# One reciprocal per head, another order of the first casts, product 5's weights by way of DRAM, two queues for the last stores

## The chip, the cores and the metric

The kernel runs on one core of a Trainium2 chip. The metric is the device time of one execution in microseconds (us), given as the median of several runs; lower is better. A profiled execution is recorded apart from those runs and has a time of its own.

## The reference

One residual layer for 512 tokens of width 1024 in float32. The normalised input goes through one combined projection; its parts feed two attention branches and two gates; the branches are projected, gated, summed and projected once more, and a normalisation ends the layer.

```python
h = rmsnorm(x, norm_g)
(q_lat, c_kv, k_rope, z_a, q_b, k_b, v_b, z_b,
 q_idx, k_idx, w_idx, gate_a, gate_b) = split(h @ w_in)      # 1024 x 5576
# branch a: 8 heads, latent queries (rank 384), latent keys and values (rank 256), rotary part
q  = rmsnorm(q_lat, g_q_lat) @ w_uq ;  kv = rmsnorm(c_kv, g_kv_lat) @ w_ukv
y_a = softmax(chunk_causal(q k^T * scale)) v * silu(z_a)
# branch b: 8 heads; an indexer scores the keys, each query keeps the 128 best admissible ones
score = sum_h relu(q_idx k_idx^T) * w_idx ;  idx = top_k(score, 128)
y_b = softmax(q_b k_b[idx]^T * scale + rel_bias) v_b[idx] * silu(z_b)
merged = sigmoid(gate_a) * (y_a @ w_o_a) + sigmoid(gate_b) * (y_b @ w_o_b)
out = rmsnorm(x + merged @ w_out, final_g)
```

## The kernel before

**Numbers in two parts.** Each float32 operand of an important product is split into a high part, rounded to the matmul's input type fp32r, and a low part, the rest. A product is three matmuls: high by high, high by low, low by high (`mm3`). The helpers record the instructions, so many steps share a line: matmuls L395, transposes of probabilities L412, casts to the high part L297 on ScalarE (ACT), low parts and other two-tensor steps L323 on VectorE (DVE) or L325 on GpSimd (POOL), activations L306 (ACT), scalings by a value per row L353 (DVE), L356 (POOL) or L306 (ACT), DMAs of the SyncE queue (SP) L422.

**Weights.** Every weight comes from DRAM once, through SP's one queue in program order, into a raw tile (four of 128x1024 float32, named `raw`; at the start `s_er`). ACT makes its high part and DVE or POOL its low part in one of 73 slots of 128x512 (`s_w`, `s_wo`, and others by their use); then the raw tile is free for the next load.

**The order of the work.** A scheduler of the kernel's own, the class `Flow`, decides it when the program is built. The work is written as threads (Python generators) that yield a `Step` (engine options, reads, writes), a `Get` (a buffer of a pool) or an `Until` (a condition). Each thread has a priority. `Flow.run` puts down, again and again, the step that can start first by a cost model, with a bias by priority, and where a step has several engines, the one on which it ends first. The model has a line for SP's DMAs: an issue time, the time the data takes on the shared transfers, a landing time. Small random nudges are drawn from a seed, `DRAW`. What is put down is the program order of each engine; at run time engines wait for one another by semaphores only.

**The stages.** (1) x arrives transposed in blocks `s_x`; ACT scales each by the input's norm gains and makes the high part `s_xg`, DVE the low one. The first weight blocks (`s_er`: the latent and index columns q and kv) are cast to `s_w`, and PE multiplies them as the blocks of x arrive. Fifteen matmuls of zeros run ahead of the first. (2) The other columns of the projection in an order given by the string `QUEUE`, with the normalised input `s_h`. Meanwhile DVE finds the top 128 keys of each query (16 rounds of max and replace for three tiles), and the a-heads' attention runs between PE's products. (3) The b-heads in the same way, their operands moved to their partitions by DMAs (`s_op`, `qhi`, `s_pair` on the way). (4) The gated projections, and last the output projection by w_out in seven products of sums and differences of blocks instead of eight, in the order 1, 7, 2, 6, 5, 4, 3. Products 5 and 7 multiply differences of w_out's blocks: `out_job` loads a pair of blocks as one raw tile of 512 KB, subtracts (`s_wsum`), casts and makes the low part (`s_wo`), four times for product 5. (5) `finish` adds x (`s_xr`), multiplies by the final gain (`s_fg`), sums squares, and `scale_out` scales the halves of each row tile (`s_rg`) and stores them.

**A head.** `mla_head` (a) and `dsa_head` (b) have four row tiles of 128 queries with 128, 256, 384 and 512 keys. For each, the function `soft` finds the negative row maximum, exponentiates on ACT with the row sum in `accum`, and normalises:

```python
def normalise(p, mx, engs=None):
    yield Step([("DVE", 0.07, lambda: nc.vector.reciprocal(mx.tile[:, 3:4], mx.tile[:, 2:3]))], [mx], [mx])
    step = scale_by(p, p, mx[:, 3:4], engs or NORM)
```

`NORM` is DVE or POOL (a-heads), `NORM_B` DVE or ACT (b-heads). When all tiles of a head are scaled, `attend` transposes them by matmuls with an identity (L412), makes high and low parts (`s_ph`) and multiplies by the values (`vv`).

## Time and profile before

| | |
|---|---|
| median of 3 runs | 428.33 us (428.06 to 428.80) |
| the profiled execution's own time | 430.56 us |
| its span in the trace | 428.8 us |
| mean granted TensorE clock | 0.991 of full speed |
| TensorE (PE) busy | 416.8 us, 97% of the span, 2313 matmuls |
| VectorE (DVE) busy | 379.1 us, 88% |
| ScalarE (ACT) busy | 261.1 us, 61% |
| GpSimd (POOL) busy | 120.2 us, 28% |
| bytes moved by DMA | 65.89 MB, 154 GB/s on the mean |

Times in the rows of the profile are in us from the start of the span unless marked ns. A row of a timeline has start, length, engine, line, operation, output tile <- input tiles, shape, how many, and in brackets how long the engine was idle before and which step ended that. PE is the matmul stream, PEld its weight loads, SPq and ACTq the DMAs that these engines issue. A matmul's length is modelled; a busy PE isn't always one at its peak.

### The profile page before, as it was taken

How to read it: one execution, taken by the hardware profiler on the slowest of the kernel's cores; microseconds unless marked ns; L12 is line 12 of the kernel's file. 1: busy time of each engine (PE TensorE's matmuls, PEld its weight loads, DVE VectorE, ACT ScalarE, POOL GpSimd, SP SyncE). 2: the span in 40 equal slices, each digit the busy share in tenths (PEclk: the TensorE clock that was granted, in tenths of full speed). 3: DMA queues.
4: the chain of work that ended last, by engine and by line, in shares of the span. 5: the costliest groups of instructions: out<-in, count | busy, mean ns of one | idle time of the engine just before them, and what ended most of it. 6: DMA issues, size and time to landing. Idle time of an engine off the chain costs nothing.

```text
span 428.8 us, 7187 instructions
## 1 busy us (share of the span) xinstructions
PE 416.8 (97%) x2313; PEld 365.4 (85%) x2313; DVE 379.1 (88%) x851; ACT 261.1 (61%) x589; POOL 120.2 (28%) x141
## 2 busy tenths in 40 slices
PE   7999999999999999999999999999999999999994
PEld 5999978888888888878899888988898888888883
DVE  3679999999999999998777897998799867999985
ACT  5876877576373838449462768584499534436623
POOL 1045767466264678200000001110000002010552
PEclk8999999999999999999999999999999999999997
DMA  8973144635555363182443425515432897356405
GB/s 260 396 265 113 52 153 127 185 113 134 132 124 161 106 179 98 39 222 73 137 135 112 148 98 131 160 49 187 117 125 78 270 336 266 128 160 234 148 0 196
DMA packets 30277, 65.89 MB, mean 154 GB/s; under 512 B 4648, under 2 KB 5688, under 8 KB 30240
## 3 DMA queue, kind: packets, MB, share of 16 engines
q1 hardware_dynamic: 29264, 64.08, 48.3%
q0 software_dynamic: 832, 1.22, 1.0%
q8 instruction: 18, 0.29, 0.3%
q14 instruction: 19, 0.16, 0.1%
q10 hardware_dynamic: 144, 0.13, 0.1%
HBM read 50.49 MB, written 4.21 MB: 128 GB/s over the span
## 4 chain that ended last, share of the span: by engine, by line
PE 74%; DVE 13%; DMA 4%; ACT 4%; issue 2%; POOL 0%; SPq 0%; POOLq 0%; ACTq 0%; DVEq 0%
PE ps L395 66%; PE ps L412 4%; DVE s_w L323 2%; ACT s_p L306 2%; DMA raw<-w_gb 2%; DVE s_ph L323 1%; ACT s_w L297 1%; DMA qhi<-qhi 1%; DMA s_x<-xT 1%; DVE raw L323 1%; PE ps L798 1%; DVE s_tmp L323 1%; PE ps L1461 1%; PE ps L1460 1%; DVE s_y L323 1%
## 5 line engine op out<-in xcount | busy, mean ns | idle before, releaser
L395 PE MATMUL ps<-s_h,s_w 128*128 128x512 f32 (+1 forms) x732 | 169.7, 378 | 0.7 <-ACT s_pair L297 0.7
L395 PEld LDWEIGHTS ps<-s_h,s_w 128*128 128x128 f32 x732 | 127.9, 189 | 22.8 <-ACT s_pair L297 0.9
L297 ACT CAST s_w<-raw 128x512 fp32r<-128x512 f32 (+3 forms) x124 | 71.7, 593 | 24.6 <-DVE raw L323 15.9
L325 POOL TENSOR_TENSOR s_w<-raw,s_w 128x512 fp32r<-128x512 f32 (+2 forms) x38 | 46.0, 1214 | 106.8 <-ACT s_w L297 105.3
L323 DVE TENSOR_TENSOR s_w<-raw,s_w 128x512 fp32r<-128x512 f32 (+2 forms) x86 | 58.2, 689 | 5.7 <-ACT s_w L297 4.9
L395 PE MATMUL ps<-s_ys,s_w 128*128 128x512 f32 x192 | 43.7, 389 | 0.0
L395 PEld LDWEIGHTS ps<-s_ys,s_w 128*128 128x128 f32 x192 | 36.0, 188 | 7.5
L395 PE MATMUL ps<-s_w,s_xg 128*128 128x328 f32 (+1 forms) x192 | 34.0, 333 | 0.6 <-DVE s_w L323 0.3
L395 PEld LDWEIGHTS ps<-s_w,s_xg 128*128 128x128 f32 x192 | 32.5, 195 | 1.2 <-DVE s_w L323 0.7
L395 PE MATMUL ps<-s_wo,s_mg 128*128 128x512 f32 (+1 forms) x156 | 33.0, 373 | 0.0
L395 PEld LDWEIGHTS ps<-s_wo,s_mg 128*128 128x128 f32 x156 | 27.6, 188 | 5.2
L306 ACT ACTIVATE s_p<-s_p,sm 128x128 f32<-128x128 f32 (+3 forms) x53 | 27.5, 541 | 7.2 <-DVE sm L1539 6.1
L323 DVE TENSOR_TENSOR s_ph<-ps,s_ph 128x384 fp32r<-128x384 f32 (+1 forms) x48 | 27.5, 593 | 3.6 <-ACT s_ph L297 3.6
L306 ACT ACTIVATE s_p<-ps,sm 128x128 f32<-128x128 f32 (+3 forms) x32 | 16.8, 527 | 17.0 <-DVE sm L1442 16.4
L325 POOL TENSOR_TENSOR s_p<-s_bias,mask 128x384 f32<-128x384 f32 (+1 forms) x5 | 4.3, 886 | 78.1 <-DVE s_w L323 71.8
L297 ACT CAST s_ph<-ps 128x384 fp32r<-128x384 f32 (+1 forms) x48 | 23.8, 521 | 4.0 <-PE ps L412 3.8
L821 DVE MATCH_REPLACE8 mask<-sm,mask 128x384 f32<-128x384 f32 (+2 forms) x48 | 25.8, 542 | 0.0
L820 DVE MAX8 sm<-mask 128x8 f32<-128x384 f32 (+2 forms) x48 | 25.5, 548 | 0.1
L395 PE MATMUL ps<-s_ph,vv 128*128 128x512 f32 (+3 forms) x128 | 25.4, 324 | 0.0
L412 PE MATMUL ps<-ident,s_p 128*128 128x128 f32 x160 | 23.8, 273 | 0.7 <-DVE s_p L353 0.7
L412 PEld LDWEIGHTS ps<-ident,s_p 128*128 128x128 f32 x160 | 19.2, 140 | 4.2 <-DVE s_p L353 1.1
L395 PEld LDWEIGHTS ps<-s_ph,vv 128*128 128x128 f32 x128 | 20.4, 189 | 1.8
(195 smaller groups left out, 769.0 us busy)
## 6 DMA issues: line engine op xcount, KB each, us to landing
raw<-w_out SPq DMA_DIRECT2D x18, 512.0 KB, 3.9
s_op<-s_op SPq DMA_DIRECT2D x36, 128.0 KB, 4.1
raw<-w_ga SPq DMA_DIRECT2D x8, 512.0 KB, 4.0
raw<-w_gb SPq DMA_DIRECT2D x8, 512.0 KB
raw<-w_o SPq DMA_DIRECT2D x16, 256.0 KB, 4.1
s_x<-xT SPq DMA_DIRECT2D x8, 256.0 KB
s_xn<-x SPq DMA_DIRECT2D x8, 256.0 KB, 5.6
bias_scratch<-s_sig SPq DMA_DIRECT2D x8, 256.0 KB, 2.0
```

What stands on the lines that cost most here:

```text
L297: nc.scalar.copy(dst.ap, src.ap)
L306: nc.scalar.activation(dst.ap, src.ap, func, **kw)
L323: opts.append(("DVE", 0.07 + 0.00104 * x.n, lambda: nc.vector.tensor_tensor(dst.ap, x.ap, y.ap, op=op)))
L325: opts.append(("POOL", 0.15 + 0.0021 * x.n, lambda: nc.gpsimd.tensor_tensor(dst.ap, x.ap, y.ap, op=op)))
L395: nc.tensor.matmul(ps.ap, l.ap, r.ap, start=start and i == 0, stop=stop and i == len(pairs) - 1, skip_group_check=more)
L412: nc.tensor.transpose(d.ap, s.ap, ident.tile)
L798: yield pe(0.005 + n / 2400, [ps.all], [qs[h].all, ks[0].all], lambda: nc.tensor.matmul(ps.tile[:, :n], qs[h].tile[:96, TOK[i]], ks[0].til ...
L820: yield Step([("DVE", t, lambda: nc.vector.max(m8.tile, work.tile))], [m8], [work])
L821: yield Step([("DVE", t, lambda: nc.vector.match_replace(work.tile, m8.tile, work.tile, MARK))], [work], [m8])
L1460: nc.tensor.matmul(o, q0[0:96], k1[0:96], start=False, stop=False)
L1461: nc.tensor.matmul(o, q1[0:96], k0[0:96], start=False, stop=True)
```

## The change

Four edits and the constants that go with them.

- `Sums` takes the place of `normalise`. A head's four row sums go to four columns of one small tile, one reciprocal of 128x4 is made when the fourth sum is there, and then each row tile is scaled. `NORM` gets ACT as a third engine.
- The scheduler's cost model counts transfers as 1.36 times as long (`SLOW`) until the modelled 7.3 us, and costs a DMA issued by ACT apart; the seed `DRAW` goes from 0 to 55. The program comes out in another order: on ACT the first weight cast (q) stands ahead of the first block of x, and the next one (kv) ahead of the second block; on DVE the low parts follow that order. SP's loads of the first microseconds keep their order. PE has the same matmuls with other neighbours.
- `make` loads product 5's four pairs of blocks after head b1, as single blocks of 256 KB into `raw` slots (`s_raw`), subtracts in place, makes the high and the low part and stores the eight results to DRAM. `fetch_made` loads them back, 256 KB each, when product 6's weights are ready. Product 5 leaves the list of `out_job`.
- `scale_out` of the last row tile (t = 1) has three pieces: half 0 by DVE and SP; columns 128 to 512 of half 1 scaled by ACT and stored by a DMA that ACT issues itself; its columns 0 to 128 by DVE and SP.

In counts: DVE goes from 802 instructions to 758 (64 reciprocals of 128x1 become 16 of 128x4); ACT keeps 505 and POOL 146; SP goes from 255 to 275 and ACT issues one DMA more.

```diff
@@ -220,14 +220,19 @@
 
                 self.free["SP"] = s + 0.05
                 self.hw = max(self.hw, s) + (0.65 if step.ins and step.outs else 0.475)
-                self.dma = max(self.dma, self.hw + 0.65) + dur
+                self.dma = max(self.dma, self.hw + 0.65)
+
+                self.dma += dur * (SLOW if self.dma < 7.3 else 1.0)
                 end = self.dma + (2.2 if step.ins and step.outs else 1.0) + step.late
             else:
                 self.free[eng] = end = s + dur
                 if self.shares(step, eng):
                     self.port = end
-                if step.moves:
-                    self.dma = max(self.dma, end + (1.0 if eng == "POOL" else 0.8)) + step.moves
+                if step.moves and eng == "ACT":
+
+                    end += 1.8 + step.moves
+                elif step.moves:
+                    self.dma = max(self.dma, end + 1.0) + step.moves
                     end = self.dma + 1.0
             for b in step.ins:
                 b.r = b.reads[eng] = max(b.r, end)
@@ -240,7 +245,7 @@
 RAW_LAG = {"DVE": 0.125, "POOL": 0.1, "ACT": 0.1}
 BIAS = 0.01
 NUDGE = 0.01
-DRAW = 0
+DRAW = 55
 TC_ARGS = {}
 
 
@@ -1415,11 +1420,38 @@
         put(ps, t)
         done.add((br, h))
 
-    def normalise(p, mx, engs=None):
-        yield Step([("DVE", 0.07, lambda: nc.vector.reciprocal(mx.tile[:, 3:4], mx.tile[:, 2:3]))], [mx], [mx])
-        step = scale_by(p, p, mx[:, 3:4], engs or NORM)
-        step.abias = NORM_BIAS if engs else 0.0
-        yield step
+    class Sums:
+
+
+        def __init__(self, group):
+            self.group, self.have, self.done, self.left, self.buf = group, 0, False, len(group), None
+
+        def at(self, i):
+            if self.buf is None:
+                self.buf = yield Get(SMALL)
+            c = i - self.group[0]
+            return self.buf[:, c : c + 1]
+
+        def normalise(self, i, p, engs=None):
+            n = len(self.group)
+            self.have += 1
+            yield Until(lambda: self.have == n)
+            if i == self.group[0]:
+                t = self.buf.tile
+                yield Step([("DVE", 0.07, lambda: nc.vector.reciprocal(t[:, 4 : 4 + n], t[:, 0:n]))], [self.buf], [self.buf])
+                self.done = True
+            else:
+                yield Until(lambda: self.done)
+            c = 4 + i - self.group[0]
+            step = scale_by(p, p, self.buf[:, c : c + 1], engs or NORM)
+            step.abias = NORM_BIAS if engs else 0.0
+            yield step
+            self.left -= 1
+            if not self.left:
+                put(self.buf)
+
+    def sums_of_head():
+        return {i: s for s in (Sums(g) for g in GROUPS) for i in s.group}
 
     def prob_tiles(cls, cap):
         s = []
@@ -1434,17 +1466,17 @@
         yield Until(lambda: ("a", h, 0) in operands and ("a", h, 1) in operands)
         (qh, ql), (kh, kl) = operands["a", h, 0], operands["a", h, 1]
         slots, probs = yield from prob_tiles("p", 6)
-        ready = set()
+        ready, sums = set(), sums_of_head()
 
         def soft(i, ps):
             n = P * (i + 1)
             mx = yield Get(SMALL)
             yield Step([("DVE", 0.07 + 0.00104 * n, lambda: nc.vector.tensor_reduce(
                 mx.tile[:, 1:2], ps.tile[:, :n], op=ALU.max, axis=AX.X, negate=True))], [mx], [ps])
-            yield act(probs[i], ps[:, :n], AF.Exp, bias=mx[:, 1:2], scale=1.0, accum=mx[:, 2:3])
-            put(ps)
-            yield from normalise(probs[i], mx)
-            put(mx)
+            den = yield from sums[i].at(i)
+            yield act(probs[i], ps[:, :n], AF.Exp, bias=mx[:, 1:2], scale=1.0, accum=den)
+            put(ps, mx)
+            yield from sums[i].normalise(i, probs[i])
             ready.add(i)
 
         for i in ORDER:
@@ -1530,7 +1562,7 @@
         yield Until(lambda: ("b", h, 0) in operands and ("b", h, 1) in operands and h in bases)
         qb, (kh, kl) = operands["b", h, 0], operands["b", h, 1]
         slots, probs = bases[h]
-        ready = set()
+        ready, sums = set(), sums_of_head()
 
         def soft(i, ps):
             n = P * (i + 1)
@@ -1543,9 +1575,10 @@
             yield step
             put(ps)
 
-            yield act(p, p, AF.Exp, bias=mx[:, 1:2], scale=-1.0, accum=mx[:, 2:3])
-            yield from normalise(p, mx, NORM_B)
+            den = yield from sums[i].at(i)
+            yield act(p, p, AF.Exp, bias=mx[:, 1:2], scale=-1.0, accum=den)
             put(mx)
+            yield from sums[i].normalise(i, p, NORM_B)
             ready.add(i)
 
         for i in ORDER:
@@ -1705,6 +1738,48 @@
             src = a["w_out"][4 * h + 2 * g + c]
         Job(src, [512, 512], None, prep=prep)
 
+
+    store = nc.dram_tensor("made_scratch", (len(MADE) * 8, P, S), F32, kind="Internal").ap()
+
+    def made(product, k, part):
+        return store[8 * MADE.index(product) + 2 * k + part]
+
+    def make():
+        yield is_done(("b", 1))
+        for product in MADE:
+            h, g = {1: (0, 0), 2: (0, 1), 3: (1, 1), 5: (1, 0)}[product]
+            for k in range(4):
+                raw = yield slot("raw")
+                yield dma(raw.all, w_block(h, g, k))
+                if product == 5:
+                    other = yield slot("raw")
+                    yield dma(other.all, w_block(0, 0, k))
+                    yield soon(tt(raw.all, raw.all, other.all, ALU.subtract, BOTH))
+                    put(other)
+                hi = yield slot("wo")
+                lo = yield slot("wo")
+                yield act(hi.all, raw.all)
+                yield soon(lo_part(lo.all, raw.all, hi.all))
+                put(raw)
+                for part, t in enumerate((hi, lo)):
+                    yield dma(made(product, k, part), t.all.f)
+                put(hi, lo)
+                done.add(("made", product, k))
+
+    def fetch_made():
+        for product in MADE:
+            first = {5: (6, 3), 3: (4, 3), 2: (7, 3), 1: None}[product]
+            for k in range(4):
+                yield is_done(("made", product, k), "projections")
+                yield Until(lambda: first is None or first in right or first in used)
+                pair = []
+                for part in range(2):
+                    t = yield slot("wo", 32)
+                    yield dma(t.all.f, made(product, k, part))
+                    pair.append(t)
+                right[product, k] = tuple(pair)
+
+    used = set()
     xr, fg = {}, {}
 
     def final_loads():
@@ -1761,10 +1836,21 @@
         done.add(("sum", t))
         yield power(rs[:, 0:1])
         yield Until(lambda: all(("g", t, i) in done for i in range(count)))
-        for half, engs in ((0, ("DVE",)), (1, ("ACT",))):
-            x = rg[t, half].all.f
-            yield scale_by(x, x, rs[:, 0:1], engs)
-            yield dma(out[TOK[t], half * 512 : (half + 1) * 512], x)
+        if t != 1:
+            for half, engs in ((0, ("DVE",)), (1, ("ACT",))):
+                x = rg[t, half].all.f
+                yield scale_by(x, x, rs[:, 0:1], engs)
+                yield dma(out[TOK[t], half * 512 : (half + 1) * 512], x)
+            return
+
+        for half, c0, c1, eng in ((0, 0, 512, "DVE"), (1, 128, 512, "ACT"), (1, 0, 128, "DVE")):
+            x = rg[t, half].all.f[:, c0:c1]
+            yield scale_by(x, x, rs[:, 0:1], (eng,))
+            dst = out[TOK[t], half * 512 + c0 : half * 512 + c1]
+            if eng == "ACT":
+                yield Step([("ACT", 0.06, lambda: nc.scalar.dma_start(dst, x.ap))], [], bufs(x))
+            else:
+                yield dma(dst, x)
 
     def product(n, banks, left, cols, more=False):
 
@@ -1774,6 +1860,7 @@
                 x = cut(left[k], slice(cols + i * P, cols + i * P + P))
                 yield mm3(banks[i].all, x, whole(right[n, k]), k == 0 and not more, k == 3, more)
             put(*right[n, k])
+            used.add((n, k))
 
     def z_parts(z, i):
         return [(z[1], 0, 256), (z[2], 256, 512)] if i else [(z[0], 0, 512)]
@@ -1835,6 +1922,7 @@
                 for ps, c0, c1 in z_parts(z, i):
                     yield mm3(ps[:, c0:c1], x, cut(right[5, k], slice(c0, c1)), k == 0, k == 3)
             put(*right[5, k])
+            used.add((5, k))
         for k in range(4):
             put(*left3[k])
         for i in range(2):
@@ -1859,7 +1947,7 @@
             spawn(scale_out(i, 2 + i), 0)
 
 
-    outs = [(p, c) for p, n in ((1, 2), (7, 4), (2, 2), (6, 2), (5, 4), (4, 2), (3, 2)) for c in range(n)]
+    outs = [(p, c) for p, n in ((1, 2), (7, 4), (2, 2), (6, 2), (5, 4), (4, 2), (3, 2)) if p not in MADE for c in range(n)]
     for item in QUEUE.split():
         kind, n = item[:2].lower(), item[2:]
         how = proj if item[0].islower() else lambda *tile: in_pairs(tile)
@@ -1912,15 +2000,20 @@
     spawn(input_sums(), PSUMS)
     spawn(fetch_gates(), 9)
     spawn(final_loads(), 20)
+    spawn(make(), PMAKE)
+    spawn(fetch_made(), 9)
     spawn(output(), 15)
     run()
 
 
 PSQ = 0.0
 PSET = 0.0
-NORM = ('DVE', 'POOL')
+NORM = ('DVE', 'POOL', 'ACT')
 NORM_B = ('DVE', 'ACT')
 NORM_BIAS = -0.5
+MADE = (5,)
+PMAKE = 16
+GROUPS = ((0, 1, 2, 3),)
 NWARM = 15
 WARM = 0.22
 XAT = 3
@@ -1936,6 +2029,7 @@
 ORDER = [0,1,2,3]
 QUEUE = 'ga0 ga1 pe ma0 va0 ga2 za0 ma1 va1 ga3 za1 ma2 ga4 za2 ma3 ga5 za3 sb0 zb0 ga6 ga7 sb1 VB GB0 GB1 sb2 zb1 GB2 GB3 sb3 zb2 GB4 GB5 ou zb3 gb6 ou gb7 ou'
 LATE = 0.5
+SLOW = 1.36
 PSUMS = 8.0
 PCAP = 10
 SUMS_AT = ("a", 5)
```

## The prediction

> **What bounds the kernel now.** I read the page first: busy time, slices and clock.
>
> ```profile
> span 428.8 us, 7187 instructions
> PE 416.8 (97%) x2313; PEld 365.4 (85%) x2313; DVE 379.1 (88%) x851; ACT 261.1 (61%) x589; POOL 120.2 (28%) x141
> PE   7999999999999999999999999999999999999994
> PEclk8999999999999999999999999999999999999997
> ```
>
> TensorE (PE) is busy in all slices but the first and the last, at the full clock in all but the ends. The changed program issues the same 2313 matmuls in another order, so it can win or lose only where PE stands idle, runs at a lower clock, or has finished: the start, a few gaps, the tail. To find those I read the chain that ended last and then PE's waits.
>
> ```profile
> 2.11 4.50 DMA s_x<-xT
> 8.61 18.32 PE ps L395 x107
> 323.01 93.14 PE ps L395 x426
> PE ps L395 <- DMA qhi<-s_op: 0.7, 1, 0.7
> PE ps L395 <- ACT s_pair L297: 0.7, 1, 0.7
> PE ps L412 <- DVE s_p L353: 0.7, 1, 0.7
> PE ps L395 <- DVE s_pair L323: 0.5, 1, 0.5
> ```
>
> The chain (start, length, what) leaves the second transfer of x for PE at 8.61; from 323 on PE works 93 us without a break. Four single waits in between come to 2.6 us. The windows (PE, PEld, DVE, ACT, POOL busy, then granted clock, DMA share, GB/s) show what each stretch is short of:
>
> ```profile
> 4.52:7.93 3.41, 1.81 (x9) 1.35 (x9) 1.62 (x3) 2.23 (x6) 0.00 (x0) 1.00 0.99 328
> 7.93:11.34 3.41, 3.09 (x11) 2.75 (x12) 2.96 (x7) 2.63 (x6) 0.00 (x0) 0.50 1.02 387
> 11.34:14.75 3.41, 3.41 (x23) 3.41 (x22) 2.42 (x5) 2.59 (x7) 0.00 (x0) 1.00 1.05 404
> 180.00:190.00 10.00, 10.00 (x45) 8.28 (x45) 10.00 (x21) 5.05 (x9) 0.00 (x0) 1.00 0.81 200
> 280.00:290.00 10.00, 9.32 (x70) 8.57 (x70) 9.48 (x25) 8.89 (x23) 1.15 (x1) 1.00 0.18 58
> 370.00:380.00 10.00, 10.00 (x46) 8.29 (x45) 10.00 (x19) 3.63 (x6) 0.00 (x0) 1.00 0.47 158
> ```
>
> At 180 and at 370 PE and VectorE (DVE) are both full: DVE's work there is hidden, but with little room. One window at the start ran at half clock.
>
> **The start.** ScalarE (ACT) and DVE take their first steps in another order; the order of the loads stays. The timeline (start, length, engine, step, the wait ahead):
>
> ```profile
> 4.28 1.09 ACT L306 ACTIVATE s_xg<-s_x,normg 128x256 fp32r<-128x256 f32 x3 [1.61 <-DMA normg<-norm_g]
> 5.28 0.39 ACT L297 CAST s_w<-s_er 128x256 fp32r<-128x256 f32 x1
> 5.72 0.68 PE L395 MATMUL ps<-s_xg,s_w 128*128 128x256 f32 x4 [1.28 <-ACT s_w L297]
> 6.55 0.97 PE L395 MATMUL ps<-s_xg,s_w 128*128 128x384 f32 x4 [0.15 <-DVE s_w L323]
> 6.64 0.72 ACT L306 ACTIVATE s_xg<-s_x,normg 128x512 fp32r<-128x512 f32 x1 [0.97 <-DMA s_x<-xT]
> 7.27 0.45 ACT L297 CAST s_w<-s_er 128x328 fp32r<-128x328 f32 x1
> 7.77 0.52 PE L395 MATMUL ps<-s_w,s_xg 128*128 128x328 f32 x1 [0.25 <-ACT s_w L297]
> 8.06 0.49 DVE L323 TENSOR_TENSOR s_w<-s_er,s_w 128x328 fp32r<-128x328 f32 x1
> 8.61 3.14 PE L395 MATMUL ps<-s_w,s_xg 128*128 128x328 f32 x11 [0.32 <-DVE s_w L323]
> ```
>
> Before, the kv weights' cast (7.27) is queued behind the scaling of x's second block, for which ACT idles 0.97 until that block lands at 2.11 + 4.50 = 6.61. After, the cast comes ahead of that scaling. The kv weights were issued between x's first and second block, so they land by 6.61: cast at the latest 6.61 to 7.06, low part (0.49) to 7.55, against 8.55 now. PE is through with the q product at 6.55 + 0.97 = 7.52. So its kv matmuls start at 7.55 at the latest instead of 8.61, 1.06 less the one matmul (0.15, as 3.41 / 23 in the window from 11.34) already done at 7.77: 0.9. The first q cast also moves ahead of x's three pieces, whose end PE awaited; the wait of 1.28 shrinks by up to the cast's 0.39, of which I take 0.3. Sum: -1.2. It is -0.6 if the blocks that follow hold PE again (DMA runs at 0.99 to 1.05 of its share there, and no order of casts makes that faster); and -1.7 if the kv weights land half a microsecond before 6.61 and the rest keeps up.
>
> **One reciprocal per head.** A head's four row tiles had each its reciprocal and its scaling as soon as its exponential was done; now one reciprocal follows the fourth exponential, then four scalings.
>
> ```profile
> L1419 DVE RECIPROCAL sm<-sm 128x1 f32<-128x1 f32 x64 | 9.6, 155 | 1.5 <-ACT s_p L306 1.0
> L353 DVE TENSOR_SCALAR s_p<-s_p,sm 128x512 f32<-128x512 f32 x6 | 3.8, 640 | 0.1
> L306 ACT ACTIVATE s_p<-s_p,sm 128x512 f32<-128x512 f32 x10 | 7.2, 718 | 0.0
> L306 ACT ACTIVATE s_p<-s_p,sm 128x256 f32<-128x256 f32 x14 | 7.0, 500 | 1.3 <-DVE sm L1419 1.0 <-DVE sm L1539 0.2
> 280.02 1.41 DVE L353 TENSOR_SCALAR s_p<-s_p,sm 128x512 f32<-128x512 f32 x1
> 281.49 0.76 PE L412 MATMUL ps<-ident,s_p 128*128 128x128 f32 x5 [0.68 <-DVE s_p L353]
> ```
>
> 64 become 16: 48 x 0.155 = 7.4 us less on DVE. Where PE is full (180, 370) that only lengthens its lead. It pays where PE waited for DVE or for work queued behind it. At 281.49 PE waited 0.68 for a scaling that took 1.41 instead of 0.64. The queues around all four waits change with the order, so each is drawn anew. The a-heads' scalings, on DVE and GpSimd (POOL), may now go to ACT too, which was busy for 5.05 of 10 at 180. The price: a block of transposes that needs four row tiles now waits for the last exponential, 0.155 and the share of four scalings. By the ACT rows 0.72 and 0.50 for the longest and the second, and 0.6 and 0.4 at the same slope between and below, those are 2.2 us, 1.1 on two engines against 0.64 before: 0.5 later per head, if no other matmuls lie ready. In a-heads they do (PE 10.00 of 10 at 180); in b-heads mostly (9.32 of 10 at 280). I let half of the 2.6 us of waits go, -1.1 after a few tenths of new ones; ends -2.6 (all go, none come) and +2.
>
> **The product made early.** Product 5's subtractions, casts and low parts move from the last 60 us into the b-heads, and its eight results go to DRAM and come back.
>
> ```profile
> L323 DVE TENSOR_TENSOR s_wo<-s_wsum,s_wo 128x512 fp32r<-128x512 f32 x15 | 10.3, 688 | 1.8 <-ACT s_wo L297 1.7
> L297 ACT CAST s_wo<-s_wsum 128x512 fp32r<-128x512 f32 x16 | 9.9, 620 | 14.0 <-DVE s_wsum L323 14.0
> 392.00:394.00 2.00, 2.00 (x10) 1.66 (x9) 2.00 (x5) 1.04 (x2) 0.00 (x0) 1.00 0.90 343
> 394.00:396.00 2.00, 2.00 (x10) 1.68 (x9) 2.00 (x5) 1.52 (x5) 0.00 (x0) 1.00 0.05 17
> 416.66 5.80 PE L395 MATMUL ps<-s_wo,qhi 128*128 128x512 f32 x36
> ```
>
> Eight DVE or POOL steps of 0.69 (six on DVE: 4.1 us) and four casts of 0.62 (2.5) leave a stretch in which DVE was full but PE never waited: no gain. They come to a stretch with DVE at 9.48 and ACT at 8.89 of 10, where the b-heads' 32 reciprocals (5.0 us) go: covered, 0. Without that cover the 4.1 us would hold PE in part; that is in the +2 above. SyncE (SP) issues 16 loads and fetches and 8 stores in place of 4 loads; a store waits for its low part, and the b-heads' operand moves queue behind it. The DMA share of 0.18 leaves room for the bytes. The loads for the last two products now stand ahead of the final loads of x in SP's order. The fetches follow the final loads, over by 395; 256 KB at 343 GB/s are 0.76, eight 6.1, so they land by 401.1. Product 5 starts three products of 5.80 before 416.66 + 5.80 = 422.46, at 405.1. 4 us of room: 0; were they 6 late, +2.
>
> **The last store by two queues.**
>
> ```profile
> 424.52 0.72 ACT L306 ACTIVATE s_rg<-s_rg,sm 128x512 f32<-128x512 f32 x1 [1.41 <-POOL sm L373]
> 424.52 0.49 DVE L353 TENSOR_SCALAR s_rg<-s_rg,sm 128x512 f32<-128x512 f32 x1 [0.44 <-POOL sm L373]
> 425.04 0.81 SPq L422 DMA_DIRECT2D out<-s_rg  x2
> ```
>
> ACT's last scaling ends at 425.24 and SP issues its store second, by 425.85. After, ACT scales 384 columns (about 0.6, the value between 0.50 and 0.72) and issues itself, at about 425.1; that saves 0.3. But a piece of 128 columns goes to DVE and SP as a third store, and another tile's scaling (0.49) moves into DVE's chain to the last sum, while a smaller step leaves it. I take 0, ends -0.3 and +0.3. The Trainium skill (DMA: Bandwidth & Descriptors, Issuing engines are not separate DMA queues) says that DMAs of several engines end on the same 16 DMA engines, and that only the sequencer's time to issue is saved. By it the gain is at most one issue, half of the 0.81 row, and the whole sum -2.7 at best.
>
> **Sum.** -1.2 - 1.1 + 0 + 0 = -2.3, all from the profiled execution. Its own time is 430.56 (428.8 of span and 1.8 around it), 2.2 above the median of 428.33; the steps are stretches of PE time, so I take them off the median: 426.0.
>
> **Rivals.** *The gain is lost again (428.0).* At 180 DVE is full beside PE. If DVE sets PE's place there, the -1.2 of the start becomes a wait later, and the reordered gaps come out alike. For it: DVE 10.00 of 10 in the windows at 180 and 370. Against it: no wait for DVE is listed there, and DVE loses 3.7 us in the a-heads itself, more than 1.2. The rest is -0.3.
>
> *The half-clock window goes (424.5).* The window before it, 4.52 to 7.93, had PE busy for 1.81 of 3.41; with the q and kv products moved up by about 0.4 to 1, PE would be busy for some 2.5. If that is enough, 7.93 to 11.34 runs full: its 11 matmuls take 11 x 0.15 = 1.6 instead of 3.09, another -1.5. Against it: I do not see where the bound lies, and the loads may then be late instead. The Trainium skill (TensorE: Matmul & The Clock Gate, What's actually happening) says that the gate opens after a busy window of about 3.4 us, that its windows run free of the kernel and that idling closes it. The rows agree in length and in one window's delay.
>
> *Held-back scalings (slower, 429.8).* If PE has no filler in the b-heads, the 0.5 per head comes eight times, +4.0 less the start's and no gain elsewhere: 428.33 - 1.2 + 4.0 = 431.1; with filler for a third of it, 429.8. It decides from 0.15 per b-head on (1.2 / 8). For it: the wait at 281.49 is of this kind. Against it: one such wait in eight heads.
>
> *SP held by the early stores (428.8).* Eight stores each wait for a low part of 0.69 while operand moves queue behind; should half of that reach PE, as the 0.7 for qhi did, 8 x 0.69 / 2 = 2.8 on 426.0 is 428.8: no change, or slower with more than half. Against it: the order was laid out with these waits known, and ACT and PE have other work.
>
> **How the numbers follow.** About 0.2% (0.9 us) is what a measurement of this kernel can tell from no change. Forecast 0.46, gain lost 0.13, window gone 0.22, scalings held 0.13, SP held 0.06. With one term at its end at a time, the forecast reaches from 424.5 (no gaps left) to 429.1 (gaps +2). To hold 8 in 10, the range goes down to the window case with half of its remaining gaps gone too (424.5 - 1.3 = 423.2) and up to 429.5, short of the held scalings' 429.8; above lie some 0.15, below 0.04. Faster by over 0.2% (below 427.5): 0.41 of the forecast, 0.05 of the lost case, all 0.22: 0.68. Within: 0.03, 0.07, 0.01 of the held scalings, 0.03 of SP: 0.14. Slower: 0.02, 0.01, 0.12, 0.03: 0.18.
>
> **What would show it.** Right: the kv product's matmuls begin by 7.6; four gaps' sum under 2; DVE busy 7 us less; fetches land before 402 with no PE wait for s_wo; the last matmul's end 2.3 earlier and 6.3 from there to the end. Wrong: PE waits for s_p or operand moves in the b-heads, of 0.3 and more each; an unbroken PE start with equal time at 200; clock 1.00 from 4.52 on (then the window case).

## The result and the profile after

The changed kernel took 433.0 us (median of 4 runs, 430.61 to 434.68) against 428.19 for the kernel before; the ratio is 1.0103, 95% interval 1.0078 to 1.0128. It was forecast at 426.0, range 423.2 to 429.5. It is slower. Its profiled execution took 433.62 with a span of 431.8. In what follows each kernel has its ratio to the kernel before in the same series, since that one's median moves between series (428.2 to 428.9).

The page of the changed kernel (first lines), four of PE's waits, and the row of its reciprocals:

```profile
span 431.8 us, 7151 instructions
PE 418.9 (97%) x2313; PEld 366.4 (85%) x2313; DVE 377.8 (87%) x807; ACT 261.4 (61%) x586; POOL 120.5 (28%) x141
PE ps L400 <- ACT s_pair L302: 1.7, 2, 1.0
PE ps L400 <- DMA qhi<-s_op: 1.4, 1, 1.4
PE ps L400 <- DVE s_pair L328: 0.7, 1, 0.7
PE ps L803 <- DMA s_qs<-s_th: 0.4, 1, 0.4
L1441 DVE RECIPROCAL sm<-sm 128x4 f32<-128x4 f32 x16 | 2.7, 167 | 0.6 <-ACT s_p L311 0.6
```

The reciprocals fell from 9.6 to 2.7 us, but DVE's busy time only from 379.1 to 377.8. It has 44 instructions less, so four other steps came to it; where the rest of the time went is not shown. PE has no wait for a held-back scaling of any size; it has new ones for an operand move (qhi) and for a PSUM copy (s_pair). The windows say where (columns as in the prediction), first before, then changed:

```profile
0.00:10.00 10.00, 6.94 (x29) 4.87 (x30) 3.61 (x9) 5.68 (x12) 1.86 (x8) 0.90 0.81 251
270.00:280.00 10.00, 10.00 (x73) 9.56 (x72) 9.94 (x29) 5.63 (x16) 1.87 (x3) 1.00 0.48 150
290.00:300.00 10.00, 10.00 (x48) 8.35 (x48) 8.50 (x17) 4.07 (x8) 0.00 (x0) 1.00 0.57 174
310.00:320.00 10.00, 10.00 (x81) 9.83 (x80) 9.53 (x37) 8.65 (x27) 0.00 (x0) 1.00 0.41 152
```
```profile
0.00:10.00 10.00, 8.57 (x34) 7.26 (x35) 4.53 (x11) 6.57 (x15) 1.86 (x8) 1.00 0.81 273
270.00:280.00 10.00, 8.62 (x60) 7.84 (x59) 9.03 (x25) 5.13 (x15) 2.80 (x2) 1.00 0.75 215
290.00:300.00 10.00, 10.00 (x48) 8.37 (x47) 6.44 (x12) 3.98 (x8) 0.00 (x0) 1.00 0.83 293
310.00:320.00 10.00, 8.79 (x67) 8.12 (x65) 9.71 (x33) 8.51 (x25) 0.00 (x0) 1.00 0.62 220
```

PE has fewer gaps at the start. At 270 and 310 PE now stands idle; at 290 DVE is busy for only 6.44 of 10 while PE is still full.

For the comparisons below, a stretch's *loss* is the sum, over its matmuls, of the distance from the start of one to the start of the next beyond what is usual for that size (its lower quartile in the same trace, transposes counted apart: 0.227 us for 512 columns, 0.146 to 0.148 for 328). It adds up gaps and half pace, and is good to 0.1 us. The tail runs from the last matmul's end to the span's end.

| trace | 0 to 40 | 40 to 80 | 200 to 240 | 260 to 280 | 280 to 300 | 300 to 320 | tail |
|---|---|---|---|---|---|---|---|
| before, as shown | 6.1 | 0.8 | 1.9 | 0.6 | 1.4 | 0.3 | 6.3 |
| before, another execution | 5.2 | 0.8 | 0.4 | 1.1 | 0.5 | 0.4 | 6.3 |
| changed kernel | 5.1 | 2.0 | 2.4 | 2.4 | 0.3 | 2.0 | 6.9 |
| its last stores undone | 4.8 | 2.0 | 1.8 | 2.4 | 0.3 | 2.5 | 6.8 |
| its early product undone | 5.0 | 2.1 | 0.3 | 0.4 | 0.3 | 0.3 | 6.8 |
| its order, early stores on POOL | 3.5 | 2.2 | 0.6 | 1.6 | 0.4 | 0.8 | 6.8 |
| its order, early stores of 32 KB | 3.1 | 2.2 | 1.8 | 1.8 | 0.3 | 0.3 | 6.9 |

Two columns are not the early product's work, since its first load is issued at 241.6: the first goes with the moment at which the full clock begins, and 200 to 240 with one load's landing. Both differ between executions of one order (last section).

### The profile page after: what moved, and what is told of

The parts are those of the page before. It is cut to its first block, busy times and chain, and to the rows that moved or that the text cites. A ratio compares the mean times of both kernels' runs of the same rounds, so it can differ in the third digit from the quotient of the medians.

```text
span 431.8 us, 7151 instructions
## 1 busy us (share of the span) xinstructions
PE 418.9 (97%) x2313; PEld 366.4 (85%) x2313; DVE 377.8 (87%) x807; ACT 261.4 (61%) x586; POOL 120.5 (28%) x141
## 4 chain that ended last, share of the span: by engine, by line
PE 72%; DVE 10%; ACT 6%; DMA 6%; issue 3%; SPq 1%; POOLq 0%; POOL 0%; DVEq 0%; ACTq 0%
PE ps L400 64%; PE ps L417 3%; ACT s_p L311 3%; DVE s_w L328 2%; DMA qhi<-s_op 2%; DMA raw<-w_gb 2%; DVE raw L328 1%; DVE s_p L328 1%; DMA s_bias<-bias_scratch 1%; PE ps L1492 1%; PE ps L1493 1%; ACT s_w L302 1%; PE ps L1491 1%; ACT s_ph L302 1%; DMA s_qs<-s_th 1%
## 5 line engine op out<-in xcount | busy, mean ns | idle before, releaser
L330 POOL TENSOR_TENSOR s_w<-raw,s_w 128x512 fp32r<-128x512 f32 (+2 forms) x40 | 52.1, 1310 | 134.2 <-DVE s_w L328 72.1
L328 DVE TENSOR_TENSOR s_w<-raw,s_w 128x512 fp32r<-128x512 f32 (+2 forms) x84 | 54.0, 656 | 6.0 <-ACT s_w L302 5.3
L311 ACT ACTIVATE s_p<-s_p,sm 128x384 f32<-128x384 f32 (+3 forms) x53 | 28.1, 552 | 4.2 <-DVE sm L1571 3.6
L826 DVE MATCH_REPLACE8 mask<-sm,mask 128x256 f32<-128x256 f32 (+2 forms) x48 | 25.8, 540 | 0.0
L825 DVE MAX8 sm<-mask 128x8 f32<-128x256 f32 (+2 forms) x48 | 25.5, 548 | 0.3 <-POOL mask L454 0.2
L400 PE MATMUL ps<-s_lat,s_w 128*128 128x512 f32 x78 | 20.8, 398 | 0.0
```

The source lines that it names most:

```text
L311: nc.scalar.activation(dst.ap, src.ap, func, **kw)
L328: opts.append(("DVE", 0.07 + 0.00104 * x.n, lambda: nc.vector.tensor_tensor(dst.ap, x.ap, y.ap, op=op)))
L330: opts.append(("POOL", 0.15 + 0.0021 * x.n, lambda: nc.gpsimd.tensor_tensor(dst.ap, x.ap, y.ap, op=op)))
L400: nc.tensor.matmul(ps.ap, l.ap, r.ap, start=start and i == 0, stop=stop and i == len(pairs) - 1, skip_group_check=more)
L825: yield Step([("DVE", t, lambda: nc.vector.max(m8.tile, work.tile))], [m8], [work])
L826: yield Step([("DVE", t, lambda: nc.vector.match_replace(work.tile, m8.tile, work.tile, MARK))], [work], [m8])
```

## The experiments

**One part undone at a time.** Each edit is made in the changed kernel.

```diff
-MADE = (5,)
+MADE = ()
```


> The changed kernel without the product made early (product 5 is made in its turn again, all else changed). Theory 'early product': the two longest new gaps of the changed kernel's profile, 1.6 us at 278 (an operand move issued behind two stores and two loads of the early product) and 1.2 us at 311 (a PSUM copy on ACT behind casts), are its work; without it they go, 433.0 - 2.8 = 430.2 us, and no PE wait over 1 us for an operand move between 240 and 320. Theory 'order': the gaps belong to the other program order as a whole, which comes out with such gaps whatever its parts; the time stays at 432 to 434.

Measured: 428.52, ratio 0.9992 (0.9971 to 1.0013). Without the early product the slowdown is gone. DVE, ACT and PE keep the changed kernel's order up to 254 us; behind that, 130 of DVE's some 810 steps and 117 of PE's 2313 stand at other places, so this run alone doesn't part the product's work from the order that the scheduler made around it. The runs in one order below do.

```diff
-        if t != 1:
+        if True:
```


> The changed kernel with the last row tile scaled and stored as before (two halves, both issued by SP). Theory 'stores': the tail from the last matmul to the end grew from 6.3 to 6.9 us because of the third piece and the second queue; undone, 433.0 - 0.5 = 432.5 us and a tail of 6.3. Theory 'late outputs': the tail is set by eight stores of 256 KB that begin 1.7 us instead of 2.6 us before the last matmul's end and keep the DMA busy until 430; then the tail stays at 6.8 to 7.1 and the time at 433.

Measured: 433.24, ratio 1.0086 (1.0053 to 1.0118), tail 6.8. The order is the changed kernel's up to the last steps, so this is also a second look at its gaps: 260 to 280 and 300 to 320 lose the same again, 200 to 240 a little less.

```diff
-GROUPS = ((0, 1, 2, 3),)
+GROUPS = ((0,), (1,), (2,), (3,))
```


> The changed kernel with a reciprocal for each row tile again (64 of 128x1), scaled at once. Theory 'held scalings': the one reciprocal per head costs up to 0.5 us per b-head; undone, 433.0 - 2 = 431.0 us or less. Theories 'early product' and 'order': PE waits for a scaled row tile only 0.2 us in the changed kernel's profile, so 432 to 434, with 7 us more of DVE work.

Measured: 431.96, ratio 1.0065 (1.0041 to 1.0089). PE now waits 1.6 us in four places for ACT's scalings.

```diff
-DRAW = 55
-SLOW = 1.36
+DRAW = 0
+SLOW = 1.0
```


> The changed kernel with the cost model's transfer factor (1.36 to 1.0) and the seed (55 to 0) of before, the three other edits kept. Theory 'order': the seed's order is what costs; the time comes to 428.2 plus the half of the lost start, 429 to 430 us. Theory 'early product': the operand moves still queue behind the early stores and loads, 432 to 434 us, with the start's gain lost (kv product from 8.6 instead of 7.1).

Measured: 432.02, ratio 1.0061 (1.0042 to 1.0081). It loses at other places: 2.0 us from 200 to 220, ahead of the early product's first load (241.0), and 2.0 from 320 to 340, behind its last store (307.4). So whether the early product costs in this order as well is not shown; the order is also not that of the kernel before. Neither of these two edits brings back what leaving out the early product does.

**What of the early product costs.**

```diff
-                    yield soon(tt(raw.all, raw.all, other.all, ALU.subtract, BOTH))
...
-                yield act(hi.all, raw.all)
-                yield soon(lo_part(lo.all, raw.all, hi.all))
-                for part, t in enumerate((hi, lo)):
+                for part, t in enumerate((raw, other)):
                     yield dma(made(product, k, part), t.all.f)
```


> The early product's eight loads, eight stores and eight fetches stay, its subtractions, casts and low parts are left out (the raw blocks are stored in place of the parts, so product 5 multiplies other numbers). Theory 'queue': stores and loads in SP's order and on the DMA engines hold the b-heads' operand moves; the cost stays, 432 to 434 us, with a PE wait of about 1.5 us for qhi. Theory 'work': the 16 steps on DVE, POOL and ACT in the b-heads cost the 4.5 us; without them 428.5 to 429.5, as without the early product.

Measured: 429.67, ratio 1.0030 (1.0002 to 1.0058).

```diff
                 for part, t in enumerate((hi, lo)):
-                    yield dma(made(product, k, part), t.all.f)
+                    if k == 0:
+                        yield dma(made(product, k, part), t.all.f)
...
-                    yield dma(t.all.f, made(product, k, part))
+                    yield dma(t.all.f, made(product, 0, part))
```


> All the early product's loads, subtractions, casts and low parts stay, but only the first of four blocks is stored (two stores of 256 KB instead of eight) and fetched four times (product 5 multiplies other numbers). Theory 'queue': most of the cost goes with six of eight stores, 428.5 to 430.5. Theory 'work': the cost stays, 432 to 434.

Measured: 430.4, ratio 1.0022 (1.0000 to 1.0044). The two stores left stand at 270, and the wait for qhi behind them (1.6 us) stayed; the six others stood later, and the loss at 300 to 320 went. Neither part alone costs the 1.0%: the transfers without the work, and the work with the loads, the fetches and two of eight stores, each cost 0.2 to 0.3%. Both orders differ from the changed kernel's (in 79 and 28 of DVE's 807 steps), so that the two hurt together, as work that waits for transfers, is only suggested here.

```diff
-        yield is_done(("b", 1))
+        yield is_done(("b", 7))
         for product in MADE
```


> The changed kernel with the early product begun after head b7 instead of b1, in the stretch in which PE has waited for nothing and DVE has room (5.9 and 7.2 of 10 busy at 340 and 350). Both theories 'queue' and 'work' put the cost down to the b-heads: it goes, 428.0 to 429.5. A theory that the cost is the DRAM round trip as such (late fetches, outputs bunched at the end) leaves 431 to 433.

Measured: 434.89, ratio 1.0129 (1.0092 to 1.0165). The gaps of the b-heads went, as both theories said, but the time did not fall. Its PE waits:

```profile
PE ps L400 <- ACT s_wo L302: 1.9, 1, 1.9
PE ps L400 <- ACT s_w L302: 1.3, 1, 1.3
PE ps L400 <- DVE s_w L328: 1.2, 2, 1.0
```

The early product's last low part is made at 403.0 and stored at 403.7, its fetches are issued from 404.1, with nothing between that waits for the stores (so product 5 multiplies other numbers here); from 400 to 420 PE loses 4.9 us, a part of it at a clock recorded at 0.50, from 404.14 to 407.55. Begun that late, the round trip has no room.

```diff
-                    yield dma(made(product, k, part), t.all.f)
+                    step = Step([("POOL", 1.03, lambda ...: nc.gpsimd.dma_start(d, x.ap))], [], [t])
```


> The changed kernel with the eight stores of the early product issued by POOL, which is idle for 7 of 10 us and more between 240 and 320, instead of SP. Theory 'queue' in its narrow form (SP's order and its issue time of 0.5 us each hold the moves): 429 to 431. If it is the bytes on the DMA engines ahead of the moves, or the work on ACT and DVE, 432 to 434.

Measured: 428.37, ratio 0.9990 (0.9970 to 1.0011). So the early product with all its bytes can cost nothing that shows here. But the scheduler sees the change and moves 36 of DVE's steps and 77 of PE's matmuls from 278 us on, so two more runs keep the order.

**The same order on every engine.** In the first, the scheduler still plans SP stores, and only the queue that issues them is another. In the second they stay where they are and carry an eighth of the bytes. In both traces DVE, ACT and PE have the changed kernel's instructions in its order, every one.

```diff
-                    yield dma(made(product, k, part), t.all.f)
+                    step = dma(made(product, k, part), t.all.f)
+                    step.options = [("SP", ..., lambda ...: nc.gpsimd.dma_start(d, x.ap))]
+                    yield step
```


> The changed kernel's program order on every engine, with only the eight stores taken out of SP's order and issued by POOL at the place where the scheduler put them. Theory 'SP's order' (the moves behind the stores are issued later): the wait for qhi at 278 falls from 1.4 to 0.4 (1.06 us of two issues less) and the whole to 429 to 431 us. Theory 'luck of the order' (the earlier run with stores on POOL was fast because the scheduler came to another order): 432 to 434 as before.

Measured: 429.64, ratio 1.0021 (1.0003 to 1.0038).

```diff
-                    yield dma(made(product, k, part), t.all.f)
+                    step = dma(made(product, k, part), t.all.f)
+                    step.options = [("SP", ..., lambda ...: nc.sync.dma_start(d[:, :64], x.ap[:, :64]))]
+                    yield step
...
-                    yield dma(t.all.f, made(product, k, part))
+                    yield dma(t.all.f, bass.AP(bias_dram.tensor, ...))
```


> The changed kernel's program order on every engine; each of the eight stores keeps its place in SP's order but moves 32 KB instead of 256 KB (64 of 512 columns; the fetches read another region of the same size, so product 5 multiplies other numbers). Theory 'SP's order': issue times and waits stay, so 432 to 433.5 us with a wait of over 1 us for qhi near 278. Theory 'bytes' (the move waits behind 512 KB of stores on the DMA engines): the wait goes and the time falls to 429 to 431.

Measured: 428.81, ratio 1.0011 (0.9994 to 1.0027). This was a miss: the issues in SP's order stayed and the cost went. So in one order the stores' bytes on SP's queue are most of the cost: 433.0 became 428.81 without seven eighths of them, and 429.64 with all of them on another queue. Two places show how. First the changed kernel's timeline before the gap at 278:

```profile
270.02 0.46 SPq L427 DMA_DIRECT2D qhi<-s_op  x1
271.17 1.06 SPq L427 DMA_DIRECT2D made_scratch<-s_wo  x2
272.28 0.96 SPq L427 DMA_DIRECT2D s_raw<-w_out  x2
273.34 0.47 SPq L427 DMA_DIRECT2D qhi<-s_op  x1
278.23 0.73 PE L400 MATMUL ps<-s_op,qhi 128*128 128x128 f32 x4 [1.38 <-DMA qhi<-s_op]
```

Between the two moves of one operand stand two stores and two loads, 2.0 us of issues and 1 MB; the second move, issued at 273.34, landed after 4.85. With the stores small it landed after 4.24 and PE waited 1.01; with the stores on POOL it was issued 1.05 sooner after the first, and landed after 5.27:

```profile
275.66 0.73 PE L400 MATMUL ps<-s_op,qhi 128*128 128x128 f32 x4 [1.01 <-DMA qhi<-s_op]
```
```profile
274.69 0.73 PE L400 MATMUL ps<-s_op,qhi 128*128 128x128 f32 x4 [0.95 <-DMA qhi<-s_op]
```

So each remedy takes 0.4 of 1.4 there. The two loads that stay between the moves may keep the rest; no run takes them out in this order. The second place is larger. The changed kernel, before the gap at 311:

```profile
287.22 2.56 SPq L427 DMA_DIRECT2D made_scratch<-s_wo  x2
289.87 0.87 SPq L427 DMA_DIRECT2D s_raw<-w_out  x2
295.50 0.69 DVE L328 TENSOR_TENSOR s_raw<-s_raw,s_raw 128x512 f32<-128x512 f32 x1 [3.38 <-DMA s_raw<-w_out]
311.19 0.98 PE L400 MATMUL ps<-s_h,s_w 128*128 128x256 f32 x6 [1.00 <-ACT s_pair L302]
```

SP waits for the second low part (the two stores take 2.56 of its time), then issues the loads behind them; the first lands 4.65 us later. With the small stores the two take 1.95, and that load lands after 2.77. DVE runs in order, has the subtraction next, and stands for 3.38 us until the load has landed: this is the 6.44 of the window at 290. What it would have done meanwhile (bias and mask of the next head, low parts) is late from there on, ACT's casts wait for it, and the copy that frees a PSUM bank waits behind a cast: PE stops at 311. The same subtraction with small stores, and with the stores on POOL:

```profile
290.75 0.69 DVE L328 TENSOR_TENSOR s_raw<-s_raw,s_raw 128x512 f32<-128x512 f32 x1 [1.21 <-DMA s_raw<-w_out]
```
```profile
290.52 0.69 DVE L328 TENSOR_TENSOR s_raw<-s_raw,s_raw 128x512 f32<-128x512 f32 x1 [1.96 <-DMA s_raw<-w_out]
```

DVE's wait of 3.4 (3.8 in the run with the last stores undone), 2.0 and 1.2 us goes with a loss from 300 to 320 of 2.0 (2.5), 0.8 and 0.3, in one and the same order of instructions; the last run below, in this order too, adds 2.4 and 1.4.

**The reciprocals, the order and the seed.**

```diff
-MADE = (5,)
-GROUPS = ((0, 1, 2, 3),)
+MADE = ()
+GROUPS = ((0,), (1,), (2,), (3,))
```


> The changed kernel without the early product and with a reciprocal per row tile: the order of the first casts and the last stores alone, beside small moves. If the one reciprocal per head gains (48 x 0.155 = 7.4 us of DVE), this is slower than the 428.5 of the kernel without the early product alone, 429 to 430; if held scalings cost, faster, 427.5 to 428; if neither, 428.5.

Measured: 431.98, ratio 1.0081 (1.0050 to 1.0112), 3.5 us above the kernel without the early product alone. The scheduler's order differs, and 2.1 us of it are a longer tail (8.9), so this says nothing yet on reciprocals. The next keeps the order (it too is made without the early product; the lines are cut to the calls):

```diff
-nc.vector.reciprocal(t[:, 4 : 4 + n], t[:, 0:n])
+[nc.vector.reciprocal(t[:, 4 + q : 5 + q], t[:, q : q + 1]) for q in range(n)]
```


> The kernel without the early product (428.5) in the same program order on every engine, with four reciprocals of 128x1 at the place of each one of 128x4: 48 x 0.155 = 7.4 us more of DVE's time, and no scaling at another place. Theory 'DVE's time counts': 430 or more. Theory 'covered': within 0.5 of 428.5, and the 3.5 us that the kernel with a reciprocal per tile was slower came from its other order.

Measured: 428.34, ratio 0.9989 (0.9972 to 1.0006): covered. The dose was smaller than expected, though: the 64 took 5.3 us in all instead of 2.7, not 9.6, so 2.6 us of DVE's time are shown to be covered and not 7.4.

```diff
-DRAW = 0
+DRAW = 55
+SLOW = 1.36
```


> The kernel before with the seed 55 and the cost model's factor 1.36 alone: the first casts in the new order, nothing else by intent, the rest as the scheduler then orders it. Theory 'the start's gain stays': PE loses 1.2 us less in the first 20 us and the time is 1.2 lower than before, 427.3. Theory 'lost again by 80': the stretch 40 to 80 loses as much more (1.2 instead of 0.8 before, as in all runs with the new start); 428.5, no change.

This one is made in the kernel before. Measured: 436.1, ratio 1.0145 (1.0109 to 1.0181). Both theories missed. The start came as forecast (PE at the kv product by 7.22), the stretch 40 to 80 lost 2.0, and then this order lost 1.6 from 160 to 180, 4.6 from 200 to 240 and 5.2 from 380 to 420 (where the clock is recorded at 0.50 from 412.35 to 415.76). PE waited there for ACT's scalings and for weights' casts and low parts. The next is made in the kernel without the early product:

```diff
-DRAW = 55
+DRAW = 7
```


> The kernel without the early product with another seed (7 for 55), which changes nothing but the order that the scheduler comes to. If an order's luck is worth a microsecond or more, 429 to 432; if not, 428 to 429.

Measured: 435.52, ratio 1.0150 (1.0122 to 1.0179). Nothing but the nudges of at most 0.01 us in the scheduler's comparison is another, and the kernel is 7 us slower. Its longest waits:

```profile
PE ps L400 <- POOL s_wo L330: 2.5, 1, 2.5
PE ps L400 <- DVE s_ph L328: 1.9, 2, 1.1
PE ps L417 <- DVE s_p L358: 1.6, 2, 1.2
```

**The kernel before once more.** 

> The kernel before once more, for its start. In the profile at hand it lost 5.2 us of the first 10 us of PE time to gaps and one window at half clock, and that execution was 2 us above the median. Theory: the shown execution was slow at the start, and a usual one has its kv product no earlier (8.6) but loses 1 to 2 us less, which is most of the gain forecast for the start. Rival: the start is the same, and the 2 us lie elsewhere (the load of w_gb before 230).

Measured: 426.79 in that execution. Both theories hold in part (span, and the windows of the start and of the 230s):

```profile
span 425.0 us, 7187 instructions
0.00:10.00 10.00, 7.79 (x32) 6.24 (x33) 4.06 (x10) 5.84 (x13) 1.86 (x8) 1.00 0.81 262
230.00:240.00 10.00, 10.00 (x81) 9.78 (x80) 9.14 (x17) 6.58 (x13) 0.00 (x0) 1.00 0.37 110
```

The start lost 0.9 less (its kv product ran on from 7.89, not 8.6), and of the gaps from 190 to 240 in the shown trace (0.7, 0.5 and 0.7 us of waits) none is left. The two in the 230s follow the load of `w_gb`, which in the shown trace took 6.64 us to land.

**A faster version.** Without the early product, one scaling is taken from DVE's queue at the end.

```diff
-            for half, engs in ((0, ("DVE",)), (1, ("ACT",))):
+            for half, engs in ((0, ("ACT",) if t == 0 else ("DVE",)), (1, ("ACT",))):
```


> The kernel without the early product; the first row tile's half 0 is scaled by ACT instead of DVE, so that no scaling of 0.49 stands in DVE's queue between the last reduction and the last sum. The order is the same elsewhere. Scalings of the last tile come 2.05 instead of 2.47 us after the last matmul, and the time is 0.4 lower, 428.1; if the DMA's end sets the tail anyway (stores still landing), no change.

Measured: 427.2, ratio 0.9958 (0.9940 to 0.9976): faster than both kernels. The last sum comes 0.4 earlier, as meant: without the edit it stands behind the scaling,

```profile
420.28 0.49 DVE L358 TENSOR_SCALAR s_rg<-s_rg,sm 128x512 f32<-128x512 f32 x1
421.14 0.16 DVE L328 TENSOR_TENSOR sm<-sm,ssf 128x1 f32<-128x1 f32 x1
422.08 0.62 ACT L311 ACTIVATE s_rg<-s_rg,sm 128x384 f32<-128x384 f32 x1 [1.08 <-POOL sm L378]
```

2.5 us from the last matmul (419.6) to the last scalings. With it, 2.1 (418.5 to 420.62). But the tail in the traces is 6.7 against 6.8, since the output stores, closer together, keep the DMA engines busy (share 1.03 and 0.98 from 421.5 to 423.5). So 0.1 us of the gain over the 428.5 is shown, and the rest (1.2 with intervals of some 0.8) is not explained.

```diff
-        if t != 1:
+        if True:
```


> The kernel without the early product and with the first row tile's half scaled by ACT (427.2), with the last row tile's stores as before: two halves, both issued by SP. Theory 'one issue saved': the second queue gains 0.3 to 0.4 us, so 427.6 here. Theory 'same engines': the stores share the DMA engines whichever queue they come from, no difference, 427.2.

Measured: 427.05, ratio 0.9965 (0.9946 to 0.9983). The second queue gains nothing, and the faster version is seen a second time.

```diff
-                    yield dma(made(product, k, part), t.all.f)
+                    step = dma(made(product, k, part), t.all.f)
+                    step.options = [("SP", ..., lambda ...: nc.gpsimd.dma_start(d, x.ap))]
+                    yield step
...
-            for half, engs in ((0, ("DVE",)), (1, ("ACT",))):
+            for half, engs in ((0, ("ACT",) if t == 0 else ("DVE",)), (1, ("ACT",))):
```


> The changed kernel's order with the early product, its stores issued by POOL, and the first row tile's half scaled by ACT. Theory 'bytes and issues on SP's queue are the whole cost': as without the early product, 427.2 and the tail 0.3 longer by the bunched output stores, 427.5. Theory 'the loads still hold DVE' (it waited 2.0 for one with the stores on POOL, 3.4 with them on SP): 428.2 to 429.2.

Measured: 428.98, ratio 1.0011 (0.9995 to 1.0028): with its stores on POOL, the early product in this order still costs about 0.5% against the same tail without it. The loads in the middle of the b-heads' operand moves and ahead of DVE stay. In the order that the scheduler made for stores on POOL it cost nothing (0.9990 against 0.9992).

## Why the prediction was wrong

**The product made early: forecast 0, measured some 4.5 us.** This is the step that failed (1.0103 against 0.9992). I set 4.1 us of DVE steps against 5.0 us of reciprocals taken away, and the bytes against a DMA share of 0.18: sums of busy time over a stretch. (The 5.0 was also a slip: 8 of the b-heads' 32 reciprocals stay, so 24 x 0.155 = 3.7 us go.) What decided was where the waits stand: with the stores' bytes nearly gone and every instruction of DVE, ACT and PE in its place, 0.9 of the 1.0% went. I named the operand moves behind the stores (the rival "SP held", 428.8, chance 0.06): right in kind, a third of the cost (1.4 us). I did not name the queue behind the subtraction: DVE waits in order for a load that SP issues only after stores that wait for low parts. That wait alone was 3.4 us, in a stretch where DVE had been idle for 0.5 (280 to 290) and 1.5 us (290 to 300) of 10 before. The fetches cost nothing, as forecast, but not by its times: I had the last landed by 401.1, and the first landed at 401.9 and the last was issued at 401.3. The room of 4 us covered it; PE waited for none.

**The gaps: forecast -1.1, not there to be had.** The four waits of 2.6 us were those of one execution 2.2 us above the median. In another, 3.8 us shorter, PE's only wait of size after the start is 0.4 us. I took the start and the gaps off the median, though the trace's own excess over the median was made of just such waits.

**The start: forecast -1.2; the steps came, but little of the gain is the order's, and it was lost again.** The steps held:

```profile
3.94 0.41 ACT L302 CAST s_w<-s_er 128x256 fp32r<-128x256 f32 x1 [1.27 <-DMA s_er<-w_qi]
5.60 0.47 ACT L302 CAST s_w<-s_er 128x328 fp32r<-128x328 f32 x1 [0.26 <-DMA s_er<-w_kvl]
7.11 3.47 PE L400 MATMUL ps<-s_w,s_xg 128*128 128x328 f32 x12
```

The kv product begins at 7.11 and runs on; in the second trace of the kernel before it ran on from 7.89, not 8.61. How much a start loses goes first of all with the moment at which the full clock begins (last section). Of the 17 traces with this start, the eleven where it begins by 6.6 us lose 3.1 to 3.7 us to 40, and the six where it begins at 8.7 or later lose 4.4 to 5.1 (mean 4.8). The three with the old start lose 5.2, 5.2 and 6.1; in two the full clock begins late, and in the third, the trace forecast from, it came at 4.5 and fell to half again. So with a late full clock the new order gains some 0.4. Whether it also makes an early full clock likelier is not shown. And from 40 to 80 the 17 lose 1.6 to 2.2 instead of 0.8 to 0.9: PE, being earlier, waits at 55.7 and at 79.6 (0.3 and 0.6; in the page, 0.4 for the DMA of s_qs). That is the rival "gain lost again", by other waits than I named; together with the tail it fits that the kernel without the early product came out equal to the one before.

**The reciprocals: forecast mostly hidden; right as far as tested.** 2.6 us of them put back in the same order made no difference. Held-back scalings were no loss either: 0.2 us of waits.

**The tail: forecast 0, -0.3 to +0.3; measured +0.4 to +0.6.** The scaling in DVE's chain to the last sum cost 0.4, as its row said, and the step that left the chain gave nothing back. In the changed kernel output stores begin 1.7 us before the last matmul's end instead of 2.6 and fill the DMA engines until 430:

```profile
423.25 5.26 SPq L427 DMA_DIRECT2D out<-s_rg  x8
427.82 0.35 ACTq L1851 DMA_DIRECT2D out<-s_rg  x1
429.50:430.00 0.50, 0.00 (x0) 0.00 (x0) 0.00 (x0) 0.00 (x0) 0.00 (x0) 0.50 0.90 323
```

Here what the Trainium skill says (DMA: Bandwidth & Descriptors, Issuing engines are not separate DMA queues) is borne out: the store of the second queue shares the engines with the others, and undoing it changed nothing in two pairs of runs (433.24 against 433.0, 427.05 against 427.2).

**What I left out altogether: the order.** A change of the seed alone moved the kernel by 7 us, 1.6%, more than any step of the sum. An edit that the scheduler sees redraws the order from the place on where it takes effect (at 254 us without the early product, from the start with another seed), and only the runs in an unchanged order tell what a part costs.

## What to carry to other kernels

When work is moved into an idle-looking stretch, follow each of its steps into its queue: a step that waits for a load holds all that stands behind it on its engine, and a load issued behind stores can land late (4.65 against 2.77 us here). A share of busy time covers neither. Before forecasting from gaps, see whether they are in a second trace; and where a scheduler orders the program, test a part with the order held fixed, since the redrawn order alone may be worth more than the part.

## What the runs showed of the hardware

The pace of the first matmuls varies between executions of the same start, and the clock column of the windows does not show it. Two windows of the same length, of the changed kernel and of the faster version:

```profile
6.98:10.39 3.41, 3.41 (x15) 3.41 (x13) 3.09 (x7) 2.87 (x7) 0.00 (x0) 1.00 1.02 383
```
```profile
6.98:10.39 3.41, 3.41 (x24) 3.41 (x23) 2.42 (x6) 2.09 (x5) 0.00 (x0) 1.00 1.00 349
6.66 1.97 PE L400 MATMUL ps<-s_w,s_xg 128*128 128x328 f32 x12
```

Both say 1.00, but the kv product's twelve matmuls took 3.28 us from start to start in the one (7.11 to 10.39, 0.273 each) and 1.81 in the other (6.66 to 8.47, 0.151 each). 0.273 is also the spacing in the window recorded at 0.50 in the trace before (9.05 to 11.24 for eight). The traces' own records of the clock explain it: the changed kernel's first one, full speed, begins only at 10.44, the faster version's at 4.24, and the view counts the time without a record as full speed. The loss to 40 follows this moment, as given above: with the new start, 3.3 us on the mean where it comes early and 4.8 where it comes late. So what the rival of the half-clock window priced, 1.5 us, did come in eleven executions; that PE's earlier work brings it is not shown, since the same start has it or not. The Trainium skill (TensorE: Matmul & The Clock Gate, What's actually happening) has the gate's windows run free of the kernel, so that the matmul at which full speed begins varies; these two traces of one start agree.

A load of 512 KB at 220 (`w_gb`) makes a gap or not. In thirteen traces with the same order up to there (in one, four reciprocals stand for each one), it landed after 5.95 to 6.87 us in seven, which lost 1.7 to 2.4 us from 200 to 240, and after 3.7 to 4.8 in six, which lost 0.3 to 0.7. So a gap of this size can come and go with nothing changed ahead of it; 2.0 of the 5.4 us between the traces of the changed kernel and the one without the early product are this one.
